# A two-layer diffusion step on one core: its opening in a fixed order of groups, and layer 1's scan values made behind layer 0's merges

## The chip, the cores and the metric

The kernel runs on one core of one Trainium2 chip. The core has five engines with instruction streams of their own: TensorE (PE, with weight loads as PEld), VectorE (DVE), ScalarE (ACT), GpSimd (POOL) and SyncE (SP, which here only issues DMAs). The metric is the device time of one execution in microseconds; the number given for a kernel is the median of its runs.

## The reference, cut to what matters

One inference step of a backbone with two layers on T = 640 tokens (512 latents, 128 context) of width 1024, all in float32:

```python
mod = silu(cond) @ w_mod + b_mod                       # shift, scale, gate: 3 x 1024
h = rms_norm(x) * (1 + scale) + shift
u_a, g_a, u_b, g_b, u_c, g_c, m = split(h @ w_in)      # 1024 -> 7168
y_a = GLU(S5_bidir(u_a)) * silu(g_a)                   # 32 groups x 16 channels, 64 complex states
y_b = Hyena2(u_b) * silu(g_b)                          # long convolutions with implicit filters, by DFT
y_c = MultiPool(u_c) * silu(g_c)
x = x + gate * (sum(sigmoid(m_k) * (y_k @ w_br_k)) @ w_out)
```

The S5 scan of a direction has the transition a = exp(lambda dt) and the input matrix bb = k(lambda, dt) * b; it needs powers and phases of a, which depend on weights alone. The Hyena filters depend on weights alone as well: a small network with sines gives h(t), which is multiplied by a fixed decay window and transformed. After the last layer comes a norm.

## The kernel before

Every product with a large weight is made of three matmuls in a 32-bit format with fewer mantissa bits: high x high, low x high, high x low. `split` (L238, L239) makes the parts: ScalarE casts the high part, VectorE subtracts to get the low one. `linear` loads a weight chunk of 256 KB (`wr`), splits it into `wh` and `wl`, and runs the 640 tokens in two halves of 320 columns; a tile of 128 outputs from 1024 inputs is 48 matmuls of 128x320 (L261 to L263).

The program is written as one sequence; a scheduler that simulates the engines decides from it the order in which each engine gets its instructions. Semaphores follow from the tiles, and the buffers of a tag (`bufs`) bound how far a producer runs ahead.

**Opening** (`run`): the filter network `mlp` gives `fh`; x is loaded and positions added (L569). ScalarE squares x tile by tile (L582), VectorE adds the squares up (L589), and TensorE sums them over the partitions (`ssq`, L599). `filter_load` loads the windows and transform matrices. `mod_chunk` multiplies four 512 KB pieces `wm` of `w_mod` by the condition (L404, eight matmuls, buffers: 4), and `mod_turn` transposes the result (`modt`, L415). `s5_disc` and `s5_disc2` compute layer 0's scan values (`rs`, `pw`, `bb`, `pi`, `po`, `ph`) and store `pwd` and `rsd` for layer 1. `rinv` makes the inverse root mean square and spreads it over the partitions (`rr`), `make_h` normalizes and splits into `hhi` and `hlo`, one half of 320 tokens after the other. Four calls of `filter` follow: L511 gives `fw`, `fwp`; L520 and L521 multiply by the window into `hx`, `hq`; L522 and L523 add the bias `br` to one row; `fold` (L555 to L559) makes `hc`; three splits and 42 matmuls `fps` transform (L549 to L551), and the results are stored by SyncE's queue (L544).

**Each layer**: `u_a` makes the scan's four input tiles (copied to `ua`, L678, stored to `ud`, L682), `load_u` reads them back as `ug` (L689). Eight blocks of scan follow (`s5_gen`, `s5_run`: products `i` at L873 and L874, phases `tt` L919 and L922, two scans `kk` L961 and L962, result stored to `yd`). Beside each block, two or three tiles from the list `beside` run in `linear`: 12 tiles `conv_u` (short convolution: two VectorE passes, L1003 and L1005), then 4 `gate_b` (a GpSimd product, L1034), then 4 `ahead` (a tanh stored for later). Then GLU, Hyena and pooling; the merges, where layer 1's modulation (`mod_chunk`, tag "b") runs beside layer 0's tiles; the output projection; and, for layer 1, norm and filters again, the norm on GpSimd. `s5_prep` then reads `pwd` and `rsd` and makes layer 1's `bb` (GpSimd, L693 to L698), `ph` (VectorE, L846 to L851), `pi` and `po` (ScalarE, L817 to L822) and the cleared buffers `bp` and `bf` (VectorE, L832, L835).

## Time and profile before

| | value |
|---|---|
| median of 3 runs | 1531.77 us (1529.52 to 1532.61) |
| the profiled execution | 1534.17 us |
| its span in the trace | 1532.4 us |
| TensorE busy | 1435.3 us, 94% of the span, 10812 matmuls |
| VectorE busy | 1125.5 us, 73% |
| ScalarE busy | 672.0 us, 44% |
| GpSimd busy | 524.9 us, 34% |
| DMA | 178.74 MB, mean 117 GB/s |

The profiled execution is one execution; its span runs from the first recorded instruction to the last, and the 1.8 us around it belong to the start and the end. Stages of the span: opening to 107 us, the scan's input to 146 us, layer 0's scan to 341 us, GLU, Hyena and the first merges to 560 us, merges to 760 us, output projection to 809 us, layer 1's norm to 845 us, its scan's input to 886 us, its scan to 1089 us, the rest to the end. Matmul ends are modelled from pipelined starts, so a busy TensorE is not always TensorE at its peak: the distance between starts of equal matmuls tells its rate.

### The profile page before, as it was taken

To read this page: it belongs to the slowest core of one execution; us is meant where nothing else is said; L and a number is where in the kernel's file an instruction comes from. 1 tells how busy PE (TensorE), PEld (TensorE's weight loads), DVE (VectorE), ACT (ScalarE), POOL (GpSimd) and SP (SyncE) were. 2 spreads that over 40 slices of the span, in tenths; PEclk is the share of its full clock that TensorE was granted. 3 is DMA by queue.
4 is the path that set the end of the run, shared out by engine and by line. 5 is a ranking of instruction groups with operands and counts; after the bars stand their busy time and mean duration, and the time that the engine had idled before them with its cause. 6 is when DMAs were issued, how large, how long until landed. Compare 5 with 4: busy or idle time off the path is not lost.

```text
span 1532.4 us, 28365 instructions
## 1 busy us (share of the span) xinstructions
PE 1435.3 (94%) x10812; PEld 1372.2 (90%) x10812; DVE 1125.5 (73%) x1951; ACT 672.0 (44%) x1454; POOL 524.9 (34%) x473
## 2 busy tenths in 40 slices
PE   3998899999999999999998897989999999999997
PEld 1688888999999998999997787989999999999996
DVE  8996998854777795555678879896557778866665
ACT  3574545434333342344345644544443334344443
POOL 0033433500343334553323733443003444166401
PEclk9899999999999999999998899999999999999998
DMA  9535122244322246444752342223622223322154
GB/s 313 188 112 132 57 72 70 71 146 123 99 71 77 76 134 234 157 151 139 230 159 81 110 113 68 71 71 94 172 89 81 83 70 106 115 83 83 35 178 153
DMA packets 120464, 178.74 MB, mean 117 GB/s; under 512 B 33944, under 2 KB 58152, under 8 KB 119817
## 3 DMA queue, kind: packets, MB, share of 16 engines
q1 hardware_dynamic: 115737, 170.58, 36.5%
q0 software_dynamic: 1152, 5.77, 1.1%
q8 instruction: 85, 1.39, 0.4%
q10 hardware_dynamic: 3440, 0.59, 0.2%
q14 instruction: 50, 0.41, 0.1%
HBM read 152.71 MB, written 24.18 MB: 115 GB/s over the span
## 4 chain that ended last, share of the span: by engine, by line
PE 68%; DVE 15%; DMA 6%; issue 5%; ACT 3%; SPq 2%; POOL 1%; POOLq 0%; ACTq 0%; DVEq 0%
PE mm L261 15%; PE mm L263 15%; PE mm L262 15%; PE mm L333 3%; PE mm L335 3%; PE mm L334 3%; DVE wl L239 2%; PE inva L1145 1%; SPq L914 1%; DVE i L874 1%; PE invb L1145 1%; PE yp L976 1%; PE modp L404 1%; DVE vx L1003 1%; DVE hlo L665 1%
## 5 line engine op out<-in xcount | busy, mean ns | idle before, releaser
L261 PE MATMUL mm<-hhi,wh 128*128 128x320 f32 x1408 | 446.1, 318 | 15.3 <-ACT raw L996 9.0
L263 PE MATMUL mm<-hhi,wl 128*128 128x320 f32 x1408 | 440.4, 314 | 8.5 <-DVE wl L239 6.3
L262 PE MATMUL mm<-hlo,wh 128*128 128x320 f32 x1408 | 442.4, 314 | 0.5 <-DVE hlo L659 0.4
L239 DVE TENSOR_TENSOR wl<-wr,wh 128x512 fp32r<-128x512 f32 x316 | 265.9, 843 | 114.4 <-ACT wh L238 111.5
L238 ACT CAST wh<-wr 128x512 fp32r<-128x512 f32 x316 | 195.5, 619 | 269.1 <-PE mm L262 188.9
L261 PEld LDWEIGHTS mm<-hhi,wh 128*128 128x128 f32 x1408 | 269.9, 192 | 20.8 <-ACT raw L996 10.0
L263 PEld LDWEIGHTS mm<-hhi,wl 128*128 128x128 f32 x1408 | 269.5, 192 | 9.5 <-DVE wl L239 6.8
L262 PEld LDWEIGHTS mm<-hlo,wh 128*128 128x128 f32 x1408 | 270.1, 192 | 1.7 <-DVE hlo L659 1.2
L262 PE MATMUL mm<-mlo,wh 128*128 128x320 f32 x256 | 79.6, 312 | 0.5 <-DVE mlo L242 0.4
L261 PE MATMUL mm<-mhi,wh 128*128 128x320 f32 x256 | 79.1, 312 | 0.5 <-ACT wh L238 0.4
L263 PE MATMUL mm<-mhi,wl 128*128 128x320 f32 x256 | 78.8, 309 | 0.4 <-DVE wl L239 0.4
L873 POOL TENSOR_TENSOR ow<-cw,po 128x512 f32<-128x512 f32 x32 | 41.9, 1328 | 96.6 <-PE yp L976 96.5
L875 POOL TENSOR_TENSOR i<-i,i 128x1024 f32<-128x1024 f32 x16 | 40.5, 2529 | 100.6 <-DVE i L873 71.8
L1244 DVE SCALAR_TENSOR_TENSOR mth<-mth,mm 128x320 f32<-128x320 f32 x64 | 31.1, 486 | 52.5 <-PE mm L263 52.5
L1246 POOL TENSOR_TENSOR macc<-macc,mth 128x320 f32<-128x320 f32 x32 | 35.0, 1099 | 86.4 <-DVE mth L1244 86.4
L239 DVE TENSOR_TENSOR wl<-ws,wh 128x512 fp32r<-128x512 f32 x48 | 42.7, 889 | 29.7 <-ACT wh L238 28.6
L333 PE MATMUL mm<-hhi,wh 128*128 128x320 f32 x192 | 59.9, 312 | 0.0
L335 PE MATMUL mm<-hhi,wl 128*128 128x320 f32 x192 | 59.4, 309 | 0.0
L334 PE MATMUL mm<-hlo,wh 128*128 128x320 f32 x192 | 59.4, 309 | 0.0
L238 ACT CAST wh<-ws 128x512 fp32r<-128x512 f32 x48 | 29.8, 621 | 60.2 <-PE mm L334 32.3
L1052 POOL TENSOR_TENSOR ps<-pu 128x663 f32<-128x663 f32 x8 | 12.3, 1540 | 120.4 <-ACT pu L1045 120.4
L1246 POOL TENSOR_TENSOR acc<-acc,mth 128x320 f32<-128x320 f32 x32 | 37.7, 1179 | 44.4 <-DVE mth L1244 44.3
(421 smaller groups left out, 3809.9 us busy)
## 6 DMA issues: line engine op xcount, KB each, us to landing
wr<-w_in SPq DMA_DIRECT2D x224, 256.0 KB, 2.6
wm<-w_mod SPq DMA_DIRECT2D x48, 512.0 KB, 5.4
wr<-w_out SPq DMA_DIRECT2D x48, 256.0 KB, 3.0
hd<-hs SPq DMA_DIRECT2D x32, 256.0 KB, 2.3
hsr<-hd SPq DMA_DIRECT2D x32, 256.0 KB, 2.6
mt<-kd SPq DMA_DIRECT2D x128, 32.0 KB, 1.8
wr<-w_br_a SPq DMA_DIRECT2D x16, 256.0 KB, 2.6
wr<-w_br_b SPq DMA_DIRECT2D x16, 256.0 KB, 2.7
```

The costliest lines, as they stand in the source:

```text
L238: nc.scalar.copy(hi, src)
L239: nc.vector.tensor_tensor(out=lo, in0=src, in1=hi.bitcast(F32), op=ALU.subtract)
L261: nc.tensor.matmul(ps[i], wh[:, ks], at(hi, k, sl), start=(k == 0), stop=False)
L262: nc.tensor.matmul(ps[i], wh[:, ks], at(lo, k, sl), start=False, stop=False)
L263: nc.tensor.matmul(ps[i], wl[:, ks], at(hi, k, sl), start=False, stop=(k == kt - 1))
L333: nc.tensor.matmul(out, wh[:, ks], xh, start=(k == 0), stop=False)
L334: nc.tensor.matmul(out, wh[:, ks], xl, start=False, stop=False)
L335: nc.tensor.matmul(out, wl[:, ks], xh, start=False, stop=(k == 3))
L873: eng.tensor_tensor(out=out[:, r], in0=hb(r), in1=pb(0), op=ALU.mult)
L875: e.tensor_tensor(out=out, in0=out, in1=tmp, op=ALU.add)
L1244: v.scalar_tensor_tensor(out=o[:, sl], in0=th[:, sl], scalar=1.0, in1=ps, op0=ALU.add, op1=ALU.mult)
L1246: nc.gpsimd.tensor_tensor(out=acc[:, sl], in0=acc[:, sl], in1=th[:, sl], op=ALU.add)
```

## The change

- **Order of the opening.** The filters come before the modulation: filter 0, modulation 2, filter 1, modulation 3 and 0, filter 2, modulation 1, then the norm's spreading, `make_h` and filter 3. `issue_after` fixes that the instructions of one group are issued after the named matmul of the group before; it adds no semaphore.
- **Squares.** ScalarE still makes 16 squares; TensorE sums all of them (`square_pe`, 5 matmuls of one column each) into one PSUM tile, and VectorE's adds are gone.
- **Bias.** One matmul of one row adds `br` inside the PSUM sum of `fw` and of `fwp` (with a row of constants C_BR, the inverse of the window there), so L522 and L523 are gone, in both layers.
- **Clears and copies.** The clears of `bp` and `bf` go to GpSimd, in a new `s5_open`; layer 0's filter results are stored by ScalarE's queue; `make_h` takes latents and context as whole segments where it did halves; the norm ahead of layer 1 runs on VectorE.
- **Layer 1's scan values.** `s5_ahead` makes `ph`, `pi`, `po` and `bb` in four steps beside the first four merge tiles of branch 1 of layer 0, stores them to DRAM (`vd`), and `s5_prep` only loads them. The modulation pieces of the merges have 3 buffers in place of 4.
- **Tiles beside the scan.** The list begins with the convolutions of the third operand and mixes each three convolutions with two lighter tiles.
- GpSimd's DMA descriptor space is set to 8192 bytes.

```diff
+    def square_pe(self, X, kk, half, ps):
+        nc = self.nc
+        nh = HT // 64
+        sq = self.N.tile([P, HT], F32, tag="sq", name="sq", bufs=2)
+        nc.scalar.activation(sq, X[:, kk, half * HT:half * HT + HT], AF.Square)
+        for j in range(nh):
+            c = half * nh + j
+            nc.tensor.matmul(ps[:, c:c + 1], sq[:, j * 64:j * 64 + 64], self.k(C_ONE)[:, 0:1],
+                             start=(half == 0 and kk == 0 and j == 0),
+                             stop=(half == 1 and kk == KD - 1 and j == nh - 1))
...
-                                 stop=(i == len(ws) - 1))
+                                 stop=(i == len(ws) - 1 and t not in (2, 4)))
+            if t in (2, 4):
+                r = slice(0, 1) if t == 2 else slice(64, 65)
+                nc.tensor.matmul(fp if t == 4 else fw[:, t], self.k(C_BR)[r], br[r], start=False, stop=True)
...
-        v.tensor_tensor(out=hx[0:1, 2], in0=hx[0:1, 2], in1=br[0:1], op=ALU.add)
-        v.tensor_tensor(out=hq[64:65], in0=hq[64:65], in1=br[64:65], op=ALU.add)
...
-            nc.sync.dma_start(self.hd[l][o, r, :, hf], hs)
+            (nc.sync if l else nc.scalar).dma_start(self.hd[l][o, r, :, hf], hs)
...
+        self.sm0 = Q.tile([P, 2, G, H], F32, name="s5b")
+        self.nc.sync.dma_start(self.sm0, self.I['s5m'][0, :, 0:2])
...
+    def s5_ahead(self, V, step):
+        nc = self.nc
+        v = nc.vector
+        bbd, phd, pid, pod = self.vd
+        out = lambda: V.tile([P, 1024], F32, tag="vo", name="vo", bufs=1)
+        if step == 0:
+            self.vrs = V.tile([P, 8, G], F32, name="vrs")
+            nc.sync.dma_start(self.vrs, self.rsd)
+            ph = out()[:, 0:G * (NA + NBW)].rearrange("p (g m) -> p g m", g=G)
+            q = V.tile([P, G * (NA + NBW)], F32, tag="vq", name="vq", bufs=1)
+            self.phases(ph, q, self.vrs[:, 1:4])
+            nc.sync.dma_start(phd, ph)
+        elif step in (1, 2):
+            pw = V.tile([P, 1024], F32, tag="vi", name="vpw", bufs=1)[:, 0:18 * G]
+            pw = pw.rearrange("p (r e g) -> p r e g", r=2, g=G)
+            nc.sync.dma_start(pw, self.pwd)
+            t = out()[:, 0:3 * G * NT].rearrange("p (i g t) -> p i g t", i=3, g=G)
+            self.powers(*((t, None) if step == 1 else (None, t)), pw)
+            nc.sync.dma_start(pid if step == 1 else pod, t)
+        else:
+            sm = V.tile([P, 1024], F32, tag="vi", name="vsm", bufs=1)
+            nc.sync.dma_start(sm, self.I['s5m'][1, :, 0:2].rearrange("p r g h -> p (r g h)"))
+            sm = sm.rearrange("p (r g h) -> p r g h", r=2, g=G)
+            bb = out().rearrange("p (r g h) -> p r g h", r=2, g=G)
+            t = V.tile([P, G * (NA + NBW)], F32, tag="vq", name="vt", bufs=1)[:, 0:512]
+            t = t.rearrange("p (g h) -> p g h", g=G)
+            kb = lambda i: self.vrs[:, i].unsqueeze(2).to_broadcast([P, G, H])
+            for r, op in ((0, ALU.subtract), (1, ALU.add)):
+                v.tensor_tensor(out=bb[:, r], in0=kb(6), in1=sm[:, r], op=ALU.mult)
+                v.tensor_tensor(out=t, in0=kb(7), in1=sm[:, 1 - r], op=ALU.mult)
+                v.tensor_tensor(out=bb[:, r], in0=bb[:, r], in1=t, op=op)
+            nc.sync.dma_start(bbd, bb)
...
     def s5_prep(self, S):
         nc = self.nc
-        with self.pool("s5q") as Q:
-            pw = Q.tile([P, 2, 9, G], F32, name="pw")
-            nc.sync.dma_start(pw, self.pwd)
-            rs = S.tile([P, 8, G], F32, name="rsl")
-            nc.sync.dma_start(rs, self.rsd)
-            self.s5_bb(Q, S, 1, rs[:, 6], rs[:, 7])
-            self.s5_vals(S, 1, pw, rs)
+        self.bb = S.tile([P, 2, G, H], F32, name="bb")
+        self.ph = S.tile([P, G, NA + NBW], F32, name="ph")
+        self.pi = S.tile([P, 3, G, NT], F32, name="pi")
+        self.po = S.tile([P, 3, G, NT], F32, name="po")
+        for d, t in zip(self.vd, (self.bb, self.ph, self.pi, self.po)):
+            nc.sync.dma_start(t, d)
+        rs = S.tile([P, 8, G], F32, name="rsl")
+        nc.sync.dma_start(rs, self.rsd)
+        self.s5_open(S, 1, rs)
...
-                    self.setup_par()
-                    self.mod_open(0, M)
-                    self.load_x0(X, 0)
-                    dd = self.s5_disc(Q, SP)
-                    for kk in range(KD):
-                        self.square(X, kk, 0)
-                    self.load_x0(X, 1)
-                    for kk in range(KD):
-                        self.square(X, kk, 1)
                     wins = F.tile([P, 5, 512], F32, name="wins")
                     fr = F.tile([P, 3, 2, 3 * P], F32R, name="fr")
                     self.filter_load(0, F, wins, fr, fh)
-                    self.mod_turn(0, 2, self.mod_chunk(0, 2, M, "mm"), "mm")
-                    self.mod_turn(0, 3, self.mod_chunk(0, 3, M, "mm"), "mm")
-                    self.s5_disc2(Q, SP, *dd)
-                    self.mod_turn(0, 0, self.mod_chunk(0, 0, M, "mm"), "mm")
-                    rr = [r for r, _ in self.rinv((0, 1), nc.vector, "mm")]
-                    self.mod_turn(0, 1, self.mod_chunk(0, 1, M, "mm"), "mm")
+                    self.setup_par()
+                    self.mod_open(0, M)
+                    ssq = self.PS.tile([P, 512], F32, tag="mm", name="ssq", bufs=3)[0:64, 0:2 * (HT // 64)]
+                    for half in range(2):
+                        self.load_x0(X, half)
+                        for kk in range(KD):
+                            self.square_pe(X, kk, half, ssq)
+
+                    def mod(n):
+                        with tc.issue_after(self.last_f.ins):
+                            self.mod_turn(0, n, self.mod_chunk(0, n, M, "mm"), "mm")
+
+                    def filt(o, hf):
+                        with tc.issue_after(self.last_mp.ins):
+                            self.filter(0, o, hf, F)
+
+                    self.filter(0, 0, 0, F)
+                    mod(2)
+                    filt(0, 1)
+                    mod(3)
+                    self.s5_disc2(Q, SP, *self.s5_disc(Q, SP))
+                    y = self.rinv((0, 1), nc.vector, "mm", ps=ssq, spread=False)
+                    mod(0)
+                    filt(1, 0)
+                    mod(1)
+                    with tc.issue_after(self.last_mt.ins):
+                        rr = self.rspread((0, 1), y, "mm")
                 self.HP = eh.enter_context(self.pool("hp", side="left"))
                 self.new_h()
-                for half in range(2):
-                    self.make_h(0, X, half, rr[half])
-                for o in range(2):
-                    for hf in range(2):
-                        self.filter(0, o, hf, F)
+                self.make_h(0, X, ((0, LS, 0), (LS, T, 1)), rr)
+                with tc.issue_after(self.last_mt.ins):
+                    self.filter(0, 1, 1, F)
...
-                            rr = [r for r, _ in self.rinv((0, 1), nc.gpsimd, "mm")]
-                            for half in range(2):
-                                self.make_h(l + 1, X, half, rr[half])
+                            rr = self.rinv((0, 1), nc.vector, "mm")
+                            self.make_h(l + 1, X, ((0, HT, 0),), rr)
+                            self.make_h(l + 1, X, ((HT, LS, 0), (LS, T, 1)), rr[:, HT:])
...
-            beside = [lambda i=i: self.conv_u(l, i, vx[i // 4][:, i % 4, :], SP) for i in range(12)]
-            beside += [lambda i=i: self.gate_b(l, i, S, vx[2]) for i in range(4)]
-            beside += [lambda i=i: self.ahead(l, 40 + i, AF.Tanh, 0.5, SP) for i in range(4)]
+            heavy = [lambda i=i: self.conv_u(l, i, vx[i // 4][:, i % 4, :], SP) for i in (*range(8, 12), *range(8))]
+            gates = [lambda i=i: self.gate_b(l, i, S, vx[2]) for i in range(4)]
+            ahead = [lambda i=i: self.ahead(l, 40 + i, AF.Tanh, 0.5, SP) for i in range(4)]
+            light = ahead[:2] + gates + ahead[2:]
+            beside = []
+            for i in range(4):
+                h, g = heavy[3 * i:3 * i + 3], light[2 * i:2 * i + 2]
+                beside += [h[0], g[0], h[1], h[2], g[1]]
...
+                    if br == 1:
+                        self.s5_ahead(self.MM, p)
                     i = 4 * br - 4 + p
                     ln = (0, i + 4) if i < 2 else (1, i - 2)
-                    turn = (*ln, self.mod_chunk(*ln, self.MM, "b"))
+                    turn = (*ln, self.mod_chunk(*ln, self.MM, "b", 3))
```

On TensorE, at the start of the opening (`modp` is a modulation product, `fw3` and `fwp` are the filter products, `wm` its weight pieces), before:

```order
L404 MATMUL modp_358<-wm_359,cs_151 32x512 x2
L404 MATMUL modp_358<-wm_363,cs_151 32x512 x2
L404 MATMUL modp_358<-wm_367,cs_151 32x512 x2
L404 MATMUL modp_358<-wm_371,cs_151 32x512 x2
L415 MATMUL modt_377<-cst_103,mp_375 128x2 x4
L404 MATMUL modp_384<-wm_385,cs_151 32x512 x2
L404 MATMUL modp_384<-wm_389,cs_151 32x512 x2
L511 MATMUL fw3_663<-w3_349,fh0_87 128x256 x4
L511 MATMUL fwp_664<-w3_349,fh0_87 128x256
L404 MATMUL modp_384<-wm_393,cs_151 32x512 x2
L404 MATMUL modp_384<-wm_397,cs_151 32x512 x2
L511 MATMUL fw3_759<-w3_349,fh0_87 128x256 x4
```

and with the change, after the squares and filter 0's last transforms (`fps`):

```order
L552 MATMUL fps_506<-fhi_501,fr_150 128x256
L553 MATMUL fps_506<-flo_502,fr_150 128x256
L554 MATMUL fps_506<-fhi_501,fr_150 128x256
L406 MATMUL modp_521<-wm_522,cs_169 32x512 x2
L406 MATMUL modp_521<-wm_526,cs_169 32x512 x2
L406 MATMUL modp_521<-wm_530,cs_169 32x512 x2
L406 MATMUL modp_521<-wm_534,cs_169 32x512 x2
L417 MATMUL modt_540<-cst_109,mp_538 128x2 x4
L406 MATMUL modp_717<-wm_718,cs_169 32x512 x2
L406 MATMUL modp_717<-wm_722,cs_169 32x512 x2
L406 MATMUL modp_717<-wm_726,cs_169 32x512 x2
L406 MATMUL modp_717<-wm_730,cs_169 32x512 x2
```

Before, modulation 2 is ahead of the first filter product, and the next filter products stand between the pieces of modulation 3; now a whole modulation (8 products and its transposes) stands behind a whole filter.

On ScalarE in the opening (`fhp` and `fhi` are a filter's high parts, `pi`, `po` the scan's power tables), before:

```order
L238 CAST fhp<-hq 128x256
L238 CAST fhi<-hc 128x512
L817 COPY pi<-pw 64x256
L818 COPY pi<-pw 64x256
L819 COPY po<-pw 64x256
L820 COPY po<-pw 64x256
L801 DMA pwd<-pw 2304x1x32
L817 COPY pi<-pw 64x256
L818 COPY pi<-pw 64x256
```

and with the change:

```order
L849 COPY po<-pw 64x256
L851 ACTIVATE pi<-pi 128x256
L853 ACTIVATE po<-po 128x256
L599 ACTIVATE sq<-X 128x320
L956 COPY bp_1056<-bb 64x8x16
L957 COPY bp_1056<-bb 64x8x16
L958 COPY bf_1058<-bb 128x8x16
L956 COPY bp_1060<-bb 64x8x16
L957 COPY bp_1060<-bb 64x8x16
L958 COPY bf_1062<-bb 128x8x16
L240 CAST fhp<-hq 128x256
L240 CAST fhi<-hc 128x512
```

The power tables' copies, and the copies into `bp` and `bf` of layer 0's first blocks, now stand ahead of filter 0's casts.

On VectorE, where layer 1's scan begins (`wl` is a weight's low part, `ph` and `phq` the phases, `i` a block's products, `tt` its phases in use), before:

```order
L239 TENSOR_TENSOR wl<-wr,wh 128x512
L846 TENSOR_TENSOR phq<-cst,rsl 128x608
L848 TENSOR_TENSOR ph<-cst,rsl 128x608
L847 TENSOR_SCALAR phq<-phq 128x608
L239 TENSOR_TENSOR wl<-wr,wh 128x512
L849 TENSOR_TENSOR ph<-ph,phq 128x608
L239 TENSOR_TENSOR wl<-wr,wh 128x512
L850 TENSOR_TENSOR phq<-cst,rsl 128x608
L851 TENSOR_TENSOR ph<-ph,phq 128x608
L672 MEMSET ua_9719 128x8
L239 TENSOR_TENSOR wl<-wr,wh 128x512
L873 TENSOR_TENSOR i_9993<-bb,pi 128x512
```

and with the change:

```order
L241 TENSOR_TENSOR wl<-wr,wh 128x512 x2
L985 TENSOR_TENSOR tt<-ph 128x352 x2
L939 TENSOR_TENSOR i_10006<-bb,pi 128x512
L940 TENSOR_TENSOR i_10007<-bb,pi 128x512
L241 TENSOR_TENSOR wl<-wr,wh 128x512
L939 TENSOR_TENSOR i_10006<-bb,pi 128x512
L940 TENSOR_TENSOR i_10007<-bb,pi 128x512
L988 SCALAR_TENSOR_TENSOR tt<-tt 128x352 x2
```

The six operations on `ph` and `phq` no longer stand between the low parts and the first block.

## Rows read from the trace of the kernel before

**Rows 1.** The span by stretches: busy us per engine (PE, PEld, DVE, ACT, POOL), PEclk.
```profile
40.00:72.00 32.00, 30.30 (x176) 21.71 (x174) 28.50 (x79) 16.19 (x34) 0.00 (x0) 0.84 0.62 201
...
146.00:300.00 154.00, 140.67 (x1332) 136.04 (x1329) 138.71 (x187) 77.43 (x199) 64.45 (x39) 0.95 0.25 72
300.00:341.00 41.00, 41.00 (x356) 40.58 (x357) 25.84 (x36) 13.80 (x33) 6.20 (x8) 1.00 0.40 114
...
560.00:760.00 200.00, 200.00 (x1370) 183.19 (x1370) 114.01 (x205) 77.99 (x146) 80.12 (x73) 1.00 0.54 176
...
845.00:886.00 41.00, 33.36 (x240) 32.35 (x240) 32.92 (x41) 26.19 (x63) 30.10 (x21) 0.87 0.42 110
```

**Rows 2.** TensorE's waits, 0 to 107 us: total, times, longest.
```profile
PE modp L404 <- DMA wm<-w_mod: 4.3, 1, 4.3
```

**Rows 3.** Timeline of TensorE, 39 to 75 us (start, length).
```profile
39.61 1.99 PE L511 MATMUL fw<-w,fh 64*128 64x256 f32 x8
...
62.10 0.41 PE L550 MATMUL fps<-flo,fr 128*128 128x256 f32 x1
62.32 0.41 PE L551 MATMUL fps<-fhi,fr 128*128 128x256 f32 x1
...
72.20 1.92 PE L404 MATMUL modp<-wm,cs 128*32 128x512 f32 x16
...
74.75 0.28 PE L550 MATMUL fps<-flo,fr 128*128 128x256 f32 x1
74.87 0.28 PE L551 MATMUL fps<-fhi,fr 128*128 128x256 f32 x1
```

**Rows 4.** VectorE by line and shape, 0 to 146 us (busy, mean ns).
```profile
L589 DVE TENSOR_TENSOR acc<-acc,sq 128x320 f32<-128x320 f32 x12 | 5.8, 483 | 0.0
L520 DVE TENSOR_TENSOR hx<-fw,wins 128x1024 f32<-128x1024 f32 x4 | 4.9, 1216 | 0.0
...
L661 DVE SCALAR_TENSOR_TENSOR ht<-X,sg,rr 128x320 f32<-128x320 f32 x6 | 3.8, 645 | 0.2 <-PE rbc L635 0.2
...
L522 DVE TENSOR_TENSOR hx<-hx,br 1x256 f32<-1x256 f32 x4 | 1.6, 408 | 0.0
```

**Rows 5.** Timeline of ScalarE, 46 to 58 us.
```profile
50.86 0.65 ACT L817 COPY pi<-pw 64x256 f32<-64x256 f32 x1 [1.26 <-DVE pw L697]
...
56.17 0.62 ACT L238 CAST fhi<-hc 128x512 fp32r<-128x512 f32 x1
```

**Rows 6.** DMA issues of the page: count, KB each, us to landing.
```profile
wm<-w_mod SPq DMA_DIRECT2D x48, 512.0 KB, 5.4
```

**Rows 7.** Timeline of SyncE's DMA queue, two stores of scan inputs.
```profile
130.07 0.38 SPq L682 DMA_DIRECT2D ud<-ua  x1
...
879.95 0.43 SPq L682 DMA_DIRECT2D ud<-ua  x1
```

**Rows 8.** VectorE by line and shape, 146 to 300 us.
```profile
L239 DVE TENSOR_TENSOR wl<-wr,wh 128x512 fp32r<-128x512 f32 x27 | 28.2, 1044 | 1.1 <-ACT wh L238 0.9
L1003 DVE SCALAR_TENSOR_TENSOR vx<-raw,par,vx 128x642 f32<-128x642 f32 x11 | 16.4, 1493 | 1.9 <-ACT vx L1001 1.9
L1005 DVE SCALAR_TENSOR_TENSOR vx<-raw,par,vx 128x642 f32<-128x642 f32 x11 | 13.0, 1178 | 0.1
```

**Rows 9.** VectorE by line and shape, 300 to 341 us.
```profile
L239 DVE TENSOR_TENSOR wl<-wr,wh 128x512 fp32r<-128x512 f32 x9 | 6.2, 687 | 7.6 <-ACT wh L238 7.6
```

**Rows 10.** GpSimd by line and shape, 300 to 341 us.
```profile
L1034 POOL TENSOR_TENSOR vx<-vx,sgb 128x512 f32<-128x512 f32 x1 | 1.5, 1507 | 3.0 <-ACT sgb L1026 3.0
```

**Rows 11.** VectorE by line and shape, 845 to 886 us.
```profile
L239 DVE TENSOR_TENSOR wl<-wr,wh 128x512 fp32r<-128x512 f32 x8 | 11.0, 1390 | 5.5 <-ACT wh L238 5.5
...
L851 DVE TENSOR_TENSOR ph<-ph,phq 128x608 f32<-128x608 f32 x1 | 1.8, 1776 | 0.0
```

**Rows 12.** GpSimd by line and shape, 845 to 886 us.
```profile
L697 POOL TENSOR_TENSOR bb<-cb,cb 128x512 f32<-128x512 f32 x1 | 1.8, 1846 | 0.0
```

**Rows 13.** Timeline of VectorE at the end of layer 1's norm.
```profile
843.88 0.68 DVE L665 SCALAR_TENSOR_TENSOR hlo<-ht,smod,hhi 128x192 fp32r<-128x192 f32 x2
```

161 lines of the change are left out of this document (91 added, 70 removed).

## The prediction

> **What bounds the kernel now.** I read four views in this order: the span by stretches, the waits of TensorE inside the stretches that are not full, the groups by line and shape there, and the timelines where a chain of waits had to be followed. The stretches [rows 1] show two kinds of stage. From 560 to 760 us, and from 300 to 341 us, TensorE is busy all the time at the full clock: there only less matmul work could help, and the change takes hardly any away. The other stretches leave room: in the opening (40 to 72 us) the granted clock is 0.84; in the first part of layer 0's scan (146 to 300 us) VectorE is busy 138.71 of 154 us and TensorE 140.67; between layer 1's norm and its scan (845 to 886 us) TensorE works 33.36 of 41 us at a clock of 0.87, with VectorE at 32.92 and GpSimd at 30.10. The change works in just these, so each part is priced in its own stage. The profiled execution took 1534.17 us, 2.4 more than the median 1531.77; the sum is made against 1534.2, and the 2.4 is taken off at the end.
>
> **Opening: +3 us (bounds −10 and +12).** Removed from VectorE: 14 adds of squares at 0.48 us and 8 bias adds at 0.41 [rows 4], 6.8 + 3.3 us, the clears, and pieces of `make_h`. VectorE was the busiest engine here (28.50 of 32 us, [rows 1]), so if its work alone set the end, some 10 us would come back: the lower bound. The sums on TensorE cost little: they are one-column matmuls, and TensorE waits then.
>
> Against this stands the order. Before, filter products, modulation pieces and transforms interleave; now they are groups one behind the other, and each group has a chain that TensorE waits out. I follow it. TensorE's first filter product started at 39.61 us [rows 3], behind 4.3 us of waiting for modulation weights [rows 2]; without these ahead, `fw` can start at about 35. Its products take 2.5 us. On ScalarE eight power copies of 0.65 us, which ran from 50.86 to 56.17 behind the first casts [rows 5], now stand ahead of `fhp`: I put the first cast at about 48 and the end of filter 0 at 56. One more filter is then 2.5 us of products, `hx` at 1.22 us [rows 4], the bias-free `hq` and five folds at a third to half of that (I take 3.5 together), a split of 1.3 and 12 last transforms 0.12 us apart [rows 3], 1.4: about 10, and 11 with the hand-overs. A modulation is 16 records in 1.92 us [rows 3]. So modulation 2 and filter 1 end at 69, modulation 3 at 71. Modulation 0 then needs its buffers: there are four, a modulation uses all four, so its pieces can be asked for only as modulation 3's matmuls end, and a piece takes 5.4 us to land [rows 6]. TensorE waits about 5 there, filter 2 ends at 88 to 89, modulation 1 at 92, and the spread norm is there at about 94. `make_h` had 48 operations, near 0.65 us for 320 columns [rows 4]; 32 are left, some 18 us by my estimate, until 112. Three tiles of the scan's input at 7.1 us (48 matmuls; 0.12 us for 256 columns is 0.148 for 320) end at 133. Before, the last store of scan inputs was issued at 130.07 [rows 7]. That is +3. The upper bound adds two more waits like that of [rows 2] behind the other modulations. Three of the four filters are done by then, where before all four still ran partly beside `make_h`; that is why the later norm costs only 3 at the end.
>
> **Layer 0's scan: −6 us (bounds −11 and +3).** The list beside the blocks put all 12 convolutions into the first five blocks; now 8 stand there. Four convolutions less are 4 × (1.49 + 1.18) = 10.7 us of VectorE [rows 8] out of a stretch where VectorE has 15 us left and TensorE 13 [rows 1]; they go into the stretch where VectorE is idle 15 of 41 us [rows 1]. The gain can't pass the 10.7. Coming in for them are gates, whose product costs GpSimd 1.5 us for the latents [rows 10] plus the context's, and VectorE is slower beside GpSimd: a low part takes 1.04 us where GpSimd is busy (64.45 of 154 us) and 0.69 where it mostly rests [rows 8, 9]. I take half of the 10.7, rounded up.
>
> **Merges: +2 us (bounds 0 and +6).** `s5_ahead` adds about 9 us to VectorE (six operations on phases, six on `bb`) and about 6 to ScalarE. VectorE has 86 us free and ScalarE 122 [rows 1], so the work itself is hidden; if it fell late against a low part, TensorE would wait, since it is full. Three buffers for modulation pieces leave one landing of 5.4 us [rows 6] less ahead; one such landing in the open is the upper bound.
>
> **Between layer 1's norm and scan: −11 us (bounds −15 and −5).** The last part of h is made at 844.56 [rows 13]; the last store of scan inputs is issued at 879.95 [rows 7], 35 us later. Three tiles at 7.1 us take 21. In between VectorE's low parts take 1.39 us in place of 0.69, beside six operations on phases of up to 1.78 [rows 11] and GpSimd's six products of up to 1.85 [rows 12]; ScalarE makes the power copies. All of that is now in the merges, and only five loads and the first block's products stay. I put the last store at 844.6 + 21 + 3 = 868.6: −11.4. The clears, now on GpSimd, and the norm on VectorE add or take a microsecond or two.
>
> **Layer 1's scan: −6 us (bounds −11 and +3)**, by the same rows and list as layer 0's.
>
> The sum is 3 − 6 + 2 − 11 − 6 = −18: 1534.2 − 18 = 1516.2, and 1514 against the median.
>
> **Rivals.** A, slower: TensorE never comes to its full clock in the opening. The clock stood at 0.84 there already [rows 1], and equal transforms started 0.21 us apart at 62.10 and 0.12 at 74.75 [rows 3]: the lower and the upper of its two levels, 1.2 and 2.4 GHz. Groups with a wait in each give more and longer idle spans than the interleaved order did. One group at the full clock is 42 transforms at 0.12 us, 5.0, and a modulation of 1.92; at the lower level that is 6.9 us more, four times 27.7. With all other terms kept: 1514 + 27 = 1541. It turns the whole to slower from 18 us more than my +3 on. Against it: part of the transforms would lie beside VectorE's chain, so that the doubling would be covered, and [rows 1] already contains 0.84. I give it 0.11. The Trainium skill, "TensorE: Matmul & The Clock Gate", section "Loop structure matters more than you think", has a loop that waits for a DMA and falls to the half clock by that idle time; by it a modulation that waits for its pieces would be followed by slow filters, and by this case's rows the wait of 4.3 us [rows 2] and the clock of 0.84 just behind it do agree.
>
> B: the scans give nothing. GpSimd's gates come into the blocks that VectorE bounds, and all its operations there stretch as the low part does, by half [rows 8, 9]: on 138.71 us busy, 8% more would eat the 10.7. Then the two terms of −6 are 0, and the time is 1514 + 12 = 1526. For it: 1.04 against 0.69. Against it: 3 gates are only 7.5 us of GpSimd. 0.18. The Trainium skill, "SBUF — State Buffer", section "SBUF: two separate sides", says that VectorE with two inputs from SBUF and GpSimd take a common port pair as a whole, so that the one that comes later stands still until the other is done; by that rule 7.5 us of GpSimd would cost VectorE at most 7.5 of the 10.7, which leaves −3 in each scan and 1520. The low part's 1.04 us agrees with the rule's direction, but no row here shows a single blocked operation.
>
> C: all of it pays. The opening reaches its −10, each scan −11, the merges cost nothing, layer 1's entry −13: the sum is −45, 1489 against the median; half-way from the forecast lies 1501. 0.19, from 1503 down. That the change doesn't do what it says would be seen in the order of the engines, and there it does: the phases are gone from VectorE's row of work at layer 1's start, and the groups of the opening are serial.
>
> **How the numbers follow.** The forecast, 1514 with some 10 us on either side, has 0.52; A 0.11, B 0.18, C 0.19. The range goes from 1490, the end of C, to 1534, which holds B and the upper bounds of opening and merges together without A. A measurement of this kernel tells about 0.2%, 3 us, from no change. Faster by more than that: forecast, C, and nearly all of B, 0.81 once the forecast's and B's own upper ends are taken out; within 0.2%: 0.08; slower: A's 0.11.
>
> **What would show it.** Right: the last store of scan inputs of layer 0 issued at 130 to 136 us; TensorE waiting for `wm` about 5 us ahead of modulation 0; the stretch of layer 0's first five blocks shorter by 5 to 6 us and no shorter in the last three; merges at 200 us or 202; the last store of scan inputs in layer 1 within 25 us of the last part of h, with low parts near 0.7 us. Wrong: a granted clock near 0.5 from 40 to 95 us (A); low parts over 1.2 us in the first blocks with `vx` products of GpSimd beside them (B); a scan's input of layer 0 ready before 122 us (C). What would make the whole wrong is a new wait: layer 1's loads of `vd` standing behind other DMAs on SyncE's queue, so that the first block comes late although VectorE is free.

## The result, and the profile after

The changed kernel takes 1549.79 us (median of 4 runs, 1548.47 to 1550.8) against 1531.17 us: a ratio of 1.0125, 95% interval 1.011 to 1.0141. It is slower by 18.6 us where 17 us less were forecast. Its profiled execution has a span of 1549.0 us.

| | before | after |
|---|---|---|
| span | 1532.4 us | 1549.0 us |
| TensorE busy | 1435.3 us | 1470.2 us |
| VectorE busy | 1125.5 us | 1095.5 us |
| ScalarE busy | 672.0 us | 673.7 us |
| GpSimd busy | 524.9 us | 515.7 us |

VectorE lost 30 us of work, and TensorE's busy time grew by 35. To see where, I cut both executions at six events that both have, read from the timelines: the last store of scan inputs (`ud`) of each layer, the last store of scan results (`yd`), the norm's first operation ahead of layer 1 (`rx`), the end. The last row is the same changed kernel in another run (e16, below).

| | to last `ud` | scan 0, to last `yd` | to `rx` | to last `ud` | scan 1, to last `yd` | rest |
|---|---|---|---|---|---|---|
| before | 130.1 | 210.5 | 468.3 | 71.1 | 209.0 | 443.5 |
| after | 155.3 | 204.9 | 480.1 | 58.5 | 207.0 | 443.2 |
| difference | +25.2 | -5.6 | +11.8 | -12.6 | -2.0 | -0.3 |
| forecast | +3 | -6 | +2 | -11 | -6 | 0 |
| after, again | 156.5 | 206.4 | 479.8 | 58.6 | 206.9 | 442.9 |

The two executions of the changed program differ by at most 1.6 us in a stage, and the medians of its two runs by 2.1 (1549.79 and 1551.89). The gain ahead of layer 1's scan came as forecast; the opening lost 25 us and the merges 12. The opening by stretches (columns as in [rows 1]; behind the clock stand the share of time that the DMA engines were busy and GB/s), before, where three stretches are added, the first up to the last `ud` of layer 0:

```profile
0.00:130.07 130.07, 96.62 (x621) 74.36 (x621) 114.11 (x289) 69.22 (x155) 26.33 (x26) 0.93 0.59 192
72.00:107.00 35.00, 32.03 (x228) 28.04 (x226) 33.99 (x67) 25.32 (x57) 13.12 (x14) 1.00 0.24 88
107.00:146.00 39.00, 33.03 (x276) 32.22 (x277) 25.37 (x33) 19.26 (x48) 15.16 (x8) 0.99 0.58 134
```

and after:

```profile
0.00:155.33 155.33, 123.91 (x708) 100.18 (x712) 101.52 (x247) 70.01 (x146) 31.09 (x29) 0.89 0.51 161
40.00:72.00 32.00, 30.30 (x159) 24.36 (x158) 18.13 (x43) 16.52 (x34) 0.00 (x0) 0.89 0.42 133
72.00:107.00 35.00, 29.17 (x144) 17.74 (x143) 12.18 (x28) 11.62 (x22) 0.00 (x0) 0.79 0.65 222
107.00:146.00 39.00, 32.35 (x186) 30.33 (x186) 35.49 (x46) 21.70 (x50) 28.12 (x19) 0.84 0.22 68
146.00:300.00 154.00, 144.28 (x1379) 140.43 (x1378) 121.32 (x179) 77.07 (x194) 61.35 (x37) 0.99 0.33 90
560.00:760.00 200.00, 199.48 (x1324) 177.99 (x1323) 128.05 (x220) 82.16 (x155) 84.28 (x68) 1.00 0.53 169
```

VectorE's 28.50 of 32 us [rows 1] fell to 18.13, and 33.99 of 35 to 12.18. Much of that is work that only comes later, 35.49 of 39 us from 107 to 146 where 25.37 were before; up to the last `ud` VectorE works 101.52 us in place of 114.11. That is the relief, 12.6 us, and nothing uses it. TensorE's granted clock is lower than before from 72 to 146 us (0.79 and 0.84 for 1.00 and 0.99). From 146 to 300 us, a stretch that now begins 9 us ahead of the last `ud`, VectorE is no longer full; the time at 560 to 760 us looks unchanged (200.00 and 199.48 us busy). TensorE's timeline after (start, length, what ended an idle time):

```profile
36.15 2.92 PE L513 MATMUL fw<-w,fh 64*128 64x256 f32 x6
...
56.43 1.92 PE L406 MATMUL modp<-wm,cs 128*32 128x512 f32 x16
...
72.18 1.92 PE L406 MATMUL modp<-wm,cs 128*32 128x512 f32 x16
...
78.81 4.86 PE L406 MATMUL modp<-wm,cs 128*32 128x512 f32 x16 [2.92 <-DMA wm<-w_mod]
83.60 1.56 PE L513 MATMUL fw<-w,fh 64*128 64x256 f32 x6
...
86.77 0.69 PE L517 MATMUL fwp<-br,cst 1*128 1x256 f32 x2
...
97.83 1.92 PE L406 MATMUL modp<-wm,cs 128*32 128x512 f32 x16
```

Filter 0 starts at 36 and modulation 2 at 56.4, as forecast (35 and 56). Then each group is late: modulation 3 at 72.2, filter 2 at 83.6, modulation 1 only at 97.8, where one modulation was at work at 72.20 before [rows 3]. From the start of modulation 2 to the end of modulation 1 there are 43 us (56.43 to 99.75), where 36 were priced. At the end of h and behind it, VectorE's timeline and TensorE's waits (columns as in [rows 2]):

```profile
123.24 1.00 DVE L686 SCALAR_TENSOR_TENSOR hlo<-ht,smod,hhi 128x512 fp32r<-128x512 f32 x2
...
131.21 3.96 DVE L985 TENSOR_TENSOR tt<-ph 128x352 f32<-128x352 f32 x2
135.09 4.29 DVE L241 TENSOR_TENSOR wl<-wr,wh 128x512 fp32r<-128x512 f32 x2
```

```profile
PE mm L265 <- DVE wl L241: 6.4, 1, 6.4
```

The first block's phases (`tt`) stand ahead of the low parts of the scan's input tiles, which take 2.1 us each there. Times "from h" in layer 0 are counted from the start of that last row of `hlo`, 123.24 us here. The last stores of both layers, which answer to [rows 7], and layer 1's last parts of h, which answer to [rows 13]:

```profile
155.33 0.38 SPq L703 DMA_DIRECT2D ud<-ua  x1
```

```profile
898.75 0.43 SPq L703 DMA_DIRECT2D ud<-ua  x1
```

```profile
875.63 0.68 DVE L686 SCALAR_TENSOR_TENSOR hlo<-ht,smod,hhi 128x192 fp32r<-128x192 f32 x2
```

In layer 1, 22.4 us lie between the end of h (876.31) and the last store, where there were 35.4 (from 844.56): 24 were forecast. These stretches, and VectorE's low parts in them, before and after:

```profile
844.56:879.95 35.39, 27.75 (x159) 26.97 (x158) 29.79 (x36) 22.03 (x54) 27.71 (x19) 0.85 0.39 106
L239 DVE TENSOR_TENSOR wl<-wr,wh 128x512 fp32r<-128x512 f32 x7 | 10.4, 1492 | 5.5 <-ACT wh L238 5.5
```

```profile
876.31:898.75 22.44, 22.44 (x168) 22.19 (x171) 16.39 (x25) 17.51 (x46) 14.19 (x13) 1.00 0.73 192
L241 DVE TENSOR_TENSOR wl<-wr,wh 128x512 fp32r<-128x512 f32 x7 | 10.4, 1504 | 4.3 <-ACT wh L240 4.3
```

A low part takes as long as before (1.50 us for 1.49, where 0.7 were forecast). What is gone is TensorE's idle time: it is busy 22.44 of 22.44 us where it was busy 27.75 of 35.39, and its clock is 1.00 for 0.85.

### The profile page after: what moved, and what is told of

Its sections match the earlier page's. It is cut to its first block, busy times and chain, and to the rows that moved or that the text cites. A ratio compares the mean times of both kernels' runs of the same rounds, so it can differ in the third digit from the quotient of the medians.

```text
span 1549.0 us, 28648 instructions
## 1 busy us (share of the span) xinstructions
PE 1470.2 (95%) x10964; PEld 1395.5 (90%) x10964; DVE 1095.5 (71%) x1920; ACT 673.7 (43%) x1445; POOL 515.7 (33%) x460
## 4 chain that ended last, share of the span: by engine, by line
PE 67%; DVE 14%; DMA 7%; issue 5%; ACT 3%; POOL 2%; SPq 1%; POOLq 0%; DVEq 0%; ACTq 0%
PE mm L263 14%; PE mm L265 14%; PE mm L264 14%; PE mm L335 3%; PE mm L337 3%; PE mm L336 3%; DVE wl L241 2%; PE modp L406 2%; PE inva L1211 1%; PE invb L1211 1%; PE yp L1042 1%; DVE i L940 1%; SPq L980 1%; DMA kd<-kh 1%; PE fps L552 1%
## 5 line engine op out<-in xcount | busy, mean ns | idle before, releaser
L265 PEld LDWEIGHTS mm<-hhi,wl 128*128 128x128 f32 x1408 | 267.5, 190 | 12.1 <-DVE wl L241 11.6
L941 POOL TENSOR_TENSOR i<-i,i 128x1024 f32<-128x1024 f32 x16 | 44.1, 2755 | 67.7 <-DVE i L939 64.8
L1310 DVE SCALAR_TENSOR_TENSOR mth<-mth,mm 128x320 f32<-128x320 f32 x64 | 31.1, 485 | 42.4 <-PE mm L265 42.3
L678 POOL TENSOR_TENSOR ht<-X,rr 128x128 f32<-128x128 f32 (+3 forms) x10 | 12.0, 1214 | 127.8 <-DVE hlo L686 127.8
L263 PEld LDWEIGHTS mm<-mhi,wh 128*128 128x128 f32 x256 | 48.5, 191 | 6.4 <-DVE X L1334 3.1
```

Of the source, the lines that this page charges most:

```text
L263: nc.tensor.matmul(ps[i], wh[:, ks], at(hi, k, sl), start=(k == 0), stop=False)
L265: nc.tensor.matmul(ps[i], wl[:, ks], at(hi, k, sl), start=False, stop=(k == kt - 1))
L941: e.tensor_tensor(out=out, in0=out, in1=tmp, op=ALU.add)
L1310: v.scalar_tensor_tensor(out=o[:, sl], in0=th[:, sl], scalar=1.0, in1=ps, op0=ALU.add, op1=ALU.mult)
```

## The experiments

Four theories were open: that the opening's order costs (what h needs stands last), that TensorE's lower clock does, that its added matmuls do, and that the loss is in the merges or the layers. Stage numbers below are those of the table's columns. The edits are given in short form and not line by line.

**The two halves undone.** e1 puts the opening's old order back and adds the squares on VectorE; e2 keeps the opening and undoes the layers' parts.

```diff
-self.filter(0, 0, 0, F); mod(2); filt(0, 1); mod(3); ...; mod(0); filt(1, 0); mod(1)
+mod(2); mod(3); s5_disc2; mod(0); rinv; mod(1); make_h; four filters      # e1, no issue_after
-heavy = ..., light = ..., s5_ahead(...), bufs=3
+beside = conv 0-11, gates, ahead; values made in s5_prep; bufs=4          # e2
```

> The changed kernel with the opening of the kernel before: order of the groups, squares added up on VectorE, no fixed order for layer 0's scan input; the bias matmuls, the scan list, and layer 1's values behind the merges stay. Theory S (the serial opening alone makes the change slower; the other parts gain together about 8 us): the last store of layer 0's scan inputs comes back to 128 to 134 us, and the time is 1549.8 less 22 to 26, so 1524 to 1528, below the kernel before. Rival (the loss is spread: descriptor space, clears on GpSimd, results on ScalarE's queue also cost in the opening): the last store stays above 140 us and the time above 1535.

> The changed kernel with its opening, but the scan list of the kernel before, layer 1's scan values made in its own preparation again, and four modulation buffers in the merges. Theory S: the opening as slow as in the changed kernel (last store of scan inputs near 155 us), the gains of the layers gone: 1531.2 + 24, so 1554 to 1558. Rival (the new list or the values behind the merges cost more than they bring): below 1550.

e1: 1549.55 us, last `ud` at 138.9. The time is the rival's, and the store lies between the two: 16 us came back there and 9 did not, and other stages grew by nearly as much (to `rx` 482.7, the next one 63.7, scan 1 212.7). e2: 1559.6 us, above what both theories gave: the stage to `rx` is 469.7 (so the 12 us there are the layers' parts), the next one 73.0 (so is the gain), the opening 154.6. What follows: the opening loses with either set of layers, but not by order alone.

**Parts of the opening.** e3 moves filter 2 behind modulation 1; e4 adds the squares on VectorE in the change's order.

```diff
-mod(0); filt(1, 0); mod(1); rspread; make_h; filter(0, 1, 1)
+mod(0); mod(1); rspread; make_h; filter(0, 1, 0); filter(0, 1, 1)         # e3
-self.square_pe(X, kk, half, ssq)
+self.square(X, kk, half)                                                   # e4
```

> The changed kernel with one group moved: modulations 3, 0 and 1 behind each other and the norm spread, and only then filter 2, beside the making of h as filter 3 is. Theory S, in the form that h waits for modulation 1 and modulation 1 for filter 2's chain: the norm is spread about 14 us earlier (102 to about 88 us), and the time falls by 8 to 14 us, to 1536 to 1542, less than 14 since filter 2's VectorE work now lies beside h. Rival (VectorE's sum of work up to the scan's input sets the end, wherever filter 2 stands): within 3 us of 1549.8.

> The changed kernel with the squares added up on VectorE again and 20 small matmuls in place of 80. Theory S: the squares' matmuls (some 17 us of TensorE between 22 and 47 us) delay filter 0's products by little, since the filter network's result comes only at 35.6 us: the time within 3 us of 1549.8. Rival (the squares on TensorE push the first group back): 4 to 8 us faster.

e3: 1558.0 us. h ended 5 us earlier (117.9 for 123.2), and the last `ud` came at 157.1 all the same: the theory in this form falls. Filters 2 and 3 then both lie beside h and its tiles, which may be the reason; no run took them apart. e4: 1557.7 us, last `ud` at 156.9: the squares on TensorE are no loss at that store. Both totals are some 8 us above the change, which neither theory of either run had; in e4 it lies in scan 0 (209.1) and in the stage behind `rx` (63.4).

**Parts of the layers.** e5 has four modulation buffers again, e6 the norm on GpSimd, e7 h by halves.

```diff
-turn = (*ln, self.mod_chunk(*ln, self.MM, "b", 3))
+turn = (*ln, self.mod_chunk(*ln, self.MM, "b"))                            # e5, one scratch tile less
-rr = self.rinv((0, 1), nc.vector, "mm")
+rr = self.rinv((0, 1), nc.gpsimd, "mm")                                    # e6
-self.make_h(0, X, ((0, LS, 0), (LS, T, 1)), rr)
+self.make_h(0, X, ((0, HT, 0),), rr); self.make_h(0, X, ((HT, LS, 0), (LS, T, 1)), rr[:, HT:])   # e7
```

> The changed kernel with four buffers for the modulation pieces in the merges again; layer 1's values behind the merges need one scratch tile less for that, with the same twelve VectorE operations. Theory Q (SyncE's queue: with three buffers the fourth piece waits at the head of the queue until a product frees its buffer, and the output projection's weights and x wait behind it): from layer 0's last scan store to the norm's input the kernel before takes 468.3 us, the changed one 480.1; with four buffers it takes 468 to 473, and the time falls by 7 to 12 us. Rival W (the added work of layer 1's values on VectorE and ScalarE costs it): that stretch stays at 478 to 481 and the time within 3 us.

> The changed kernel with layer 1's norm (13 small operations in a chain) on GpSimd as before. Theory V (on VectorE each operation of the chain stands behind filter operations in the queue): from the norm's input to its spreading 8 to 9 us in place of 12.9, and the time 3 to 6 us less. Rival (the norm's wait is covered by the projection's last tiles and the filters' products): within 2 us.

> The changed kernel with h made by halves of 320 tokens in layer 0, the whole first half ahead of the second, as before. Theory H (the scan's input tiles can't finish before all of h, and by halves two tiles are nearly done when h is): from the end of h to the last store of scan inputs 23 to 27 us in place of 32, and the time 4 to 8 us less. Rival (VectorE's queue, where the first block's phases stand ahead of the tiles' low parts, sets that stretch): within 2 us of 32, and the time within 3 us.

e5: 1541.7 us; the stage to `rx` is 469.1. Theory Q holds, and the queue shows it. SyncE's DMA queue ahead of the output projection, before, after, and in e5 (start, time to issue, count; an issue that waits holds the queue):

```profile
711.24 1.75 SPq L401 DMA_DIRECT2D wm<-w_mod  x4
722.82 15.61 SPq L252 DMA_DIRECT2D wr<-w_out  x5
738.53 1.32 SPq L1259 DMA_DIRECT2D xo<-xT  x3
```

```profile
710.89 6.91 SPq L403 DMA_DIRECT2D wm<-w_mod  x4
...
734.19 6.91 SPq L403 DMA_DIRECT2D wm<-w_mod  x4
746.48 7.79 SPq L254 DMA_DIRECT2D wr<-w_out  x4
757.49 0.33 SPq L403 DMA_DIRECT2D wm<-w_mod  x1
...
764.20 2.23 SPq L478 DMA_DIRECT2D wins<-win  x5
770.09 1.28 SPq L1325 DMA_DIRECT2D xo<-xT  x3
```

```profile
709.86 1.75 SPq L403 DMA_DIRECT2D wm<-w_mod  x4
...
732.12 1.75 SPq L403 DMA_DIRECT2D wm<-w_mod  x4
743.71 15.60 SPq L254 DMA_DIRECT2D wr<-w_out  x5
759.41 1.32 SPq L1325 DMA_DIRECT2D xo<-xT  x3
```

With three buffers four pieces in a row take 6.91 us to issue in place of 1.75, the last chunk's fourth piece waits until 757.49, the projection's further weights and the windows stand behind it, and x is asked for at 770 us, after the projection's products have begun. TensorE then waits; ahead of that, each modulation is cut in two, its last quarter inside the next tile:

```profile
716.38 1.05 PE L406 MATMUL modp<-wm,cs 128*32 128x512 f32 x4
...
773.94 0.41 PE L263 MATMUL mm<-mhi,wh 128*128 128x320 f32 x1 [2.81 <-DVE X L1334]
```

The busy share of 560 to 760 us did not show it, yet nearly half of the loss lies there: a modulation comes every 23.30 us (710.89 to 734.19) where it was every 22.26 in e5 (709.86 to 732.12). Counted from layer 0's last `yd`, the last modulation starts 5.2 us later than in e5 (396.2 us for 391.0), and `rx` 11.0 later. e6: 1553.6 us; from `rx` to the start of the spreading (`rdg`) 7.4 us in place of 12.9 (theory V: 8 to 9), but the next part took 52.0 for 45.6, so nothing came of it. e7: 1548.7 us; from h to the last `ud` 18.0 us for 32.1, with h itself at 135.0 for 123.2. In both the wait moved by one place.

**The old opening with the layers' parts.** e8 is e1 with e5, e6, e7 together and filter results on SyncE's queue again.

```diff
+open_undone, halves, norm on gpsimd, four buffers
-(nc.sync if l else nc.scalar).dma_start(self.hd[l][o, r, :, hf], hs)
+nc.sync.dma_start(self.hd[l][o, r, :, hf], hs)
```

> The opening of the kernel before (groups, squares, h by halves, filter results on SyncE's queue), with the change's scan list, layer 1's values behind the merges with four buffers, and layer 1's norm on GpSimd. If the pieces add as the stages say (scan list -6 and -2, values behind the merges -17, merges and projection +1 to +5 with four buffers, norm 0): 1531 - 20 to 24, so 1507 to 1511. Rival (the order in which the scheduler puts the engines moves with every edit, by more than these pieces, as in the run with the opening undone): 1525 or more.

e8: 1527.7 us, ratio 0.998 (0.9964 to 0.9995). Its last `ud` is at 137.5, still 7 later than before: something that it shares with the change, and not the order, costs in the opening. What it shares are the bias matmuls, the clears and the descriptor space.

**Clock, queue, order.** e9 keeps TensorE busy, e10 queues the first block behind the low parts, e11 puts all modulations first.

```diff
+for _ in range(14): matmul(p3[:, 0:256], fr[...], fr[...], start=True, stop=True)   # e9, per filter; 32 ahead of mod(0)
+with issue_after(last wl of u_a): g = self.s5_gen(0, 0, S)                           # e10
-self.filter(0, 0, 0, F); mod(2); filt(0, 1); mod(3); ...; mod(0); filt(1, 0); mod(1)
+mod(2); mod(3); ...; mod(0); mod(1); rspread; make_h; four filters                   # e11
```

> The changed kernel with filler matmuls on TensorE in the opening: 14 behind each filter's products and 32 ahead of modulation 0, all into PSUM tiles that are overwritten afterwards; the output is unchanged. Theory C (TensorE's lower clock stretches the opening: granted 0.89, 0.79 and 0.84 from 40 to 146 us against 0.84, 1.00 and 0.99 before): the clock comes above 0.95 from 56 to 107 us, each filter takes 2 us less, the last store of scan inputs comes 5 to 10 us earlier and the time is 1540 to 1545. Rival D (the chain through VectorE, ScalarE and the queues sets the pace, and a transform is done before its successor is ready): the clock rises, the last store stays within 3 us of 155 and the time within 3 us of 1549.8.

> The changed kernel with the first scan block's VectorE operations (products and phases) queued behind the last low part of the scan's input tiles. Theory V (the first block stands ahead of the low parts on VectorE, and GpSimd slows both): from the end of h to the last store 22 to 26 us in place of 32; the first block is then late by a part of that, and the time falls by 3 to 8 us. Rival (the first block's values are needed at the same moment, so the wait moves from the input to the scan): that stretch shortens, and the stretch from the last store to layer 0's last scan store grows by as much; the time within 3 us.

> The changed kernel with all four modulations ahead of the filters, then the norm spread, and all four filters beside the making of h; squares by TensorE and all else as in the change. Theory O (what h needs stands last in the change's order; the filters are needed only by Hyena): the norm is spread by 75 to 80 us, the last store of scan inputs at 132 to 142, the time 1528 to 1537. Rival (groups in a fixed order lose wherever they stand, since nothing interleaves): the last store above 148 us and the time above 1542.

e9: 1553.1 us. The clock did rise:

```profile
40.00:72.00 32.00, 31.06 (x197) 24.22 (x200) 18.99 (x47) 17.34 (x35) 0.00 (x0) 1.00 0.44 137
72.00:107.00 35.00, 32.77 (x199) 22.88 (x192) 15.22 (x33) 12.80 (x24) 2.77 (x2) 0.92 0.62 218
107.00:146.00 39.00, 33.28 (x216) 32.10 (x216) 34.24 (x45) 23.27 (x55) 24.47 (x18) 0.94 0.27 77
```

and the last `ud` came 4.5 us earlier (150.8), less than theory C said and more than D did; the total did not follow. The fillers take TensorE's time as well, so the 4.5 are a net gain. e10: 1553.9 us; 29.2 us for 32.1 behind h, and scan 0 longer by 3.3: this fits the rival, though that stage differs by 1.6 between two executions alone. e11: last `ud` at 140.3, 15 us earlier, as theory O said, though the total is the rival's, 1550.7: scan 0 takes 210.7, to `rx` 483.3 and scan 1 210.1. The programs' texts are the same there as in the change; their order on the engines is not.

**The last ten microseconds.** The kernels e13 and e14 go on from e11.

```diff
-self.square_pe(X, kk, half, ssq)
+self.square(X, kk, half)                                                             # e13
-matmul(fp if t == 4 else fw[:, t], self.k(C_BR)[r], br[r], start=False, stop=True)
+v.tensor_tensor(out=hx[0:1, 2], in0=hx[0:1, 2], in1=br[0:1], op=ALU.add)             # e14, and hq
```

> The run with all modulations ahead of the filters, and the squares added up on VectorE again. There the last store of scan inputs came at 140.3 us, 10 later than in the kernel before, with TensorE busy 35.0 of 35 and 39.0 of 39 us from 72 to 146. Theory P (with the modulations ahead, TensorE's own work bounds the opening, and the squares' matmuls, some 17 us where the kernel before has 4, are now on its path): the last store at 130 to 136 us and 4 to 10 us less time than that run. Rival (those matmuls lie in TensorE's idle time ahead of the modulations, as they did ahead of the filters): within 2 us of 140.

> As the run before this one, and the bias added on VectorE again (two small operations for a filter) in place of two one-row matmuls of 0.7 to 1.2 us. Theory P: 1 to 4 us earlier at the last store than in that run. Rival: VectorE's adds cost as much, within 1.5 us.

e13: 1539.0 us, last `ud` at 140.7: the rival holds for the opening (the squares' sums cost it nothing), and the 12 us came in the other stages. e14: 1529.5 us, last `ud` at 130.3, as before the change. The bias matmuls held the ten microseconds; far more than the 1 to 4 expected. e14 still has the clears on GpSimd, and e12 and e15 below have the smaller descriptor space with a last `ud` at 129.4 and 129.8, so neither of these costs there. The last `ud` in e11, e13 and e14:

```profile
140.27 0.38 SPq L703 DMA_DIRECT2D ud<-ua  x1
```

```profile
140.73 0.39 SPq L703 DMA_DIRECT2D ud<-ua  x1
```

```profile
130.29 0.39 SPq L702 DMA_DIRECT2D ud<-ua  x1
```

TensorE's timeline of one filter in e13 and in e14:

```profile
78.52 1.56 PE L513 MATMUL fw<-w,fh 64*128 64x256 f32 x6
80.00 0.69 PE L517 MATMUL fw<-br,cst 1*128 1x256 f32 x2
80.63 0.70 PE L513 MATMUL fw<-w,fh 64*128 64x256 f32 x2
...
83.18 0.70 PE L513 MATMUL fwp<-w,fh 64*128 64x256 f32 x2
83.81 0.69 PE L517 MATMUL fwp<-br,cst 1*128 1x256 f32 x2
```

```profile
76.32 1.99 PE L513 MATMUL fw<-w,fh 64*128 64x256 f32 x8
...
81.48 0.70 PE L513 MATMUL fwp<-w,fh 64*128 64x256 f32 x2
```

and from 72 to 107 us in both:

```profile
72.00:107.00 35.00, 35.00 (x196) 30.20 (x195) 27.60 (x48) 18.59 (x39) 4.74 (x4) 0.87 0.19 69
```

```profile
72.00:107.00 35.00, 34.21 (x225) 31.22 (x225) 31.18 (x58) 21.35 (x43) 5.07 (x4) 0.99 0.29 89
```

The matmul of one row takes 0.69 us, as long as one of 64 rows beside it (0.70) and longer than the 0.41 us of the add that it replaced [rows 4]. The first product group lasts 2.81 us with it (78.52 to 81.33) and 1.99 without, 0.82 more; the second, 1.32 (83.18 to 84.50) and 0.70, 0.62 more. Four filters with both are 5.8 us by these rows, on an engine that was busy 35.00 of 35 us. The clock, 0.87 with them and 0.99 without, may be a part of the rest, which no run took apart.

**What is worth keeping.** e12 and e15 start from the kernel before, e16 is the changed kernel again, without an edit.

```diff
+s5_ahead beside branch 1, four buffers, s5_prep loads, descriptor space 8192         # e15
+the new scan list as well                                                             # e12
```

> The kernel before, its opening untouched, with two parts of the change: the new scan list, and layer 1's values behind the merges, with four modulation buffers (and the smaller descriptor space that makes room for them). By the stages of the earlier runs: scan list -2 to -6 in layer 0 and -2 to 0 in layer 1, merges and projection +1, norm to scan input -11 to -13: 1513 to 1519. Rival (the scheduler's order shifts with each edit by as much, as in the combined run): 1525 or more.

> The kernel before with layer 1's values behind the merges alone (four buffers, scan list as before). If the list brings what the stages say, 4 us in layer 0 and 2 to 3 in layer 1, this is 5 to 8 us above the 1517.8 of the run with both: 1522 to 1526. Rival (the list brings nothing beyond the scatter of the stages): 1516 to 1519.

> The changed kernel once more, unchanged, for a second profiled execution: how far the stages of one program differ between two executions. If stages repeat within 2 us, the differences of 3 us and more between programs stand; if they scatter by 5, only those of the opening, the merges and layer 1's entry do.

e12: 1517.8 us, ratio 0.99 (0.9877 to 0.9922). e15: 1516.6 us, ratio 0.9907 (0.9891 to 0.9924), stages 129.8, 207.9, 469.9, 58.2, 206.6, 443.1. Both beat both kernels, and they don't differ: the list brings nothing that these runs can tell, scan 0 being 206.7 with it and 207.9 without. In both, scan 0 is shorter than the 210.5 before, though e15 changes nothing in layer 0's scan. e16: 1551.9 us, stages in the first table.

## Why the prediction was wrong, step by step

- **Opening, +3 us: it was +25.2. This step failed.** In the forecast's own terms, modulation 1 ended at 99.75 us for 92, h at 124.2 for 112, and the last store came 31.1 us behind it for 21, with 6.4 us of waiting for a low part: 22 us more than the forecast's 133. The runs show two wrong terms in this. First, the chain was followed to the last group, but the cost at the end was taken as 3 on the ground that filters done early need not be done later. e11 shows that the filters have room beside h and its tiles, and that the modulations, on which h rests, do not: putting them ahead gave 15 us. The groups were also slower than priced, some of it at the lower clock: filter 2 takes 14.2 us until modulation 1 starts (83.60 to 97.83) where 11 were allowed. Second, the bias adds were booked as 3.3 us off VectorE and as nothing on TensorE. Filter 2's products with them run from 83.60 to 87.46, 3.9 us where 2.5 were allowed, and the matmuls cost 10.4 us at the last store (e13 to e14, in e11's order; in the change's own order no run took them out). VectorE's relief, 12.6 us, was worth nothing there: e13 gives the squares back to VectorE and has its last `ud` 0.4 us later. The squares' price on TensorE, nothing, was right.
- **Rival A, the clock, 27 us:** the granted clock did fall to 0.79, which is time at the lower of the two levels, but holding it up (e9) gave 4.5 us, a sixth of the price. The price took all four groups at the lower level. In the trace of the change, from 36 us to the last `ud`, 59 of the filters' transforms follow each other 0.21 us apart and 86 of them 0.12 (before: 22 and 127), and 29 matmuls of the scan's tiles 0.27 apart in place of 0.15 (before: 6). By these counts, which is an estimate, the lower level costs some 9 us here and 3 before. The Trainium skill, "TensorE: Matmul & The Clock Gate", section "Loop structure matters more than you think", has the direction (a loop that waits for a DMA falls to the half clock), and the trace agrees: 2.92 us of waiting for `wm`, and 0.79 around it. Filter 1's transforms, from 64.66 us on, step 0.21 apart as well, with no wait for `wm` ahead of them. The clock is not what decided.
- **Scans, -6 and -6: -5.6 (-4.1 in e16) and -2.0** in the stages, but of these little is the list's: e15 without it and e12 with it are alike. The forecast's sign did show, the first five blocks 6.4 us shorter (132.2 us from the last `ud` to the fifth block's store for 138.6) and the last three no shorter, yet e12 and e15 differ by only 1.0 there (135.8 and 136.8): that the first scan's -6 came out is mostly luck. Rival B's time was right in that the list gives nothing; its reason, contention by GpSimd, was not tried.
- **Merges, +2 (0 to 6): +11.8.** The added work is hidden, as said (e5 keeps it and takes 469.1 us where 468.3 were before). The bound failed: "one landing in the open" counted only one wait for a piece, and neither that each modulation's last piece now comes late (5.2 us by the last modulation) nor what stands behind it on SyncE's queue. That is 11.0 us, by one buffer.
- **Norm to scan input, -11: -12.6.** Right in size, and by taking the work away, which e15 does alone (58.2 us for 71.1). The means was another than forecast: low parts near 0.7 us did not come (1.50), but VectorE has 16.39 us of work there for 29.79, and TensorE, which waited 7.6 us for low and high parts before, doesn't wait for them any more. The norm on VectorE cost 5.5 us in its own chain (12.9 for 7.4) and gave them back behind it (45.6 for 52.0, e6).
- **The range** ended at 1534 and A's own at 1541: no case held two losses at once. Layer 1's values alone, on the kernel before, give 1516.6 us (e15), near the 1514 forecast; this is luck, since one part brings what five were counted for. C's 1489 was taken from the profiled execution; against the median its sum gives 1487.

Open: why scan 0, the merges and scan 1 differ by 2 to 4 us between programs whose text is the same there (e1, e4, e11, e13, and scan 0 in e15). Their engine orders differ, and no run fixed an order alone.

## What to carry to other kernels

Follow what the next stage needs first, and put that first: relief on an engine buys nothing when the inputs of the next stage stand behind chains of something that is needed later. When work moves to another engine, price it on the engine that gets it, by the length that its instruction has there, in the stage where that engine is full. When a buffer is taken away from a transfer, list what stands behind that transfer on its queue; the loss can lie a stage later, at the next thing that the queue carries.

## What the runs showed of the hardware

A matmul's length did not follow its rows: with 256 columns one row took 0.69 us and 64 rows 0.70, and inside a group the one of one row added 0.82. And a wait on a queue is paid by what stands behind it, or not at all. The 5.2 us more to issue four pieces (6.91 for 1.75) were nearly covered: the projection's next weights came 12.3 us behind the first piece (734.19 to 746.48) for 11.6 in e5. Then the queue stood still for 3.2 us until the last piece (754.27 to 757.49), with weights and windows behind it, and x was asked for 35.9 us behind the first piece, where it was 27.3 before and in e5. TensorE showed 199.48 of 200 us busy in the stretch in which this began.
